# First part of a streaming encoder step: range checks placed by the scheduler, sample modulation and one weight's high halves on GpSimd

## The chip, the cores and the metric

The kernel runs on one core of one Trainium2 chip. The metric is the device time of one execution in microseconds. The core has five engines that run side by side, each through its own list of instructions in order: TensorE (PE in the profile), VectorE (DVE), ScalarE (ACT), GpSimd (POOL) and SyncE (SP, which only issues DMAs here). They wait for each other through semaphores.

## The reference

One layer of a hybrid encoder, for 1024 tokens of a prompt and 8 groups of 16 sample tokens (1152 tokens in all, model width 1024):

```python
mod = jax.nn.silu(c) @ w_ada + b_ada
shift, scale, gate = jnp.split(mod[:, None, :], 3, axis=-1)
h = rms_norm(x, norm_g) * (1 + scale) + shift
proj = h @ w_in
q, k, v, z_att, z_ssd, xbc, dt_raw, gates = jnp.split(proj, IN_SPLITS, axis=-1)
```

Attention over chunks with bands, a state-space scan and merge gates follow, and at the end an output projection and a residual add. The change lies in the part that makes `h` and the first pieces of `proj`.

## The kernel before

Matrix products run in half precision with both operands split in a high half (the value rounded to f16) and a low half (what the rounding left), so each product is three matmuls. Range checks go with that: `level` (L689) squares a tile on ScalarE and keeps a sum per row, and the sums are looked at only at the very end of the kernel. Nothing else waits for a `level`, except the reuse of the buffer that it reads.

The first part works through the model width in eighths, k = 0 to 7, in transposed form (width on the partitions, 1152 tokens along the row). Its steps for one k are:

- TensorE multiplies the conditioning by a slice of `w_ada` (`mod_a`, L1102), ScalarE copies the result out of PSUM (`mod_copy`, L1127), TensorE brings it into columns (`mod_b`, L1108), and ScalarE adds biases (`mod_c`, L1138 and L1139). Now shift and scale of this eighth are there, one column for the prompt and eight for the samples.
- VectorE normalises the tokens (`norm_x`, L1147). ScalarE applies scale and shift to the 1024 prompt tokens twice: as high half in f16 (`h_hi`, L1160) and in f32 (`h_rest`, L1165).
- For the 128 sample tokens the scale differs by group, so two tensor-tensor operations with broadcast columns do it (`h_samples`, L1156 and L1157). ScalarE rounds them to the high half (`h_smp`, L1169).
- VectorE takes the low half of all tokens (`h_low`, L1172: f32 minus high half).
- TensorE multiplies (`z_mm`, L1179, nine matmuls for each k) for the first projection, whose weight halves come from L1185 (ScalarE) and L1188 (VectorE).

Rounds k = 3, 4, 5 also split the three parts of the second weight: high halves by `w_high` (L1226, ScalarE), low halves by `w_low2` (L1232, VectorE), followed by a `level` of the raw part.

The second weight feeds `dense_tok` (L1023 to L1025): for each block of 128 tokens, eight triples of matmuls, one for each k. A triple needs the high and low halves of `h` for its k and the weight part that holds its columns. Blocks end in L1464 to L1470 (copies out of PSUM, squares, sums for the norms of q and k). GpSimd works out those norms (L1497, L654 to L659) and scales q and k (L1501), and TensorE transposes them (L1521). Splits of later weights are L697 (ScalarE) and L698 (VectorE); L679 and L1269 are loads of raw weights by SP.

The order on each engine is not the order of the code. A class `Order` goes through all instructions with a table of costs and gives out, for each engine, a fixed order. Instructions whose names are in `pinned` keep the written order on their engine; `late` puts them there, and the whole first part is written with `late`. Names in `fill` are put behind others:

```python
u["at"] = u["i"] + self.FILL * (u["ins"][0].name in self.fill) - self.FAST * u["fast"]
```

with FILL = 600 places of the written order; among the instructions that could go, the one with the smallest `at` is taken. The costs know nothing of one engine slowing another.

Of the kernel before, what the change touches and what calls it, by code (L numbers as in the profile page):

```python
# [13 lines left out]
AF = mybir.ActivationFunctionType  # L14
ALU = mybir.AluOpType

P = 128
# [3 lines left out]
NB = 8  # L21
NS = 16
# [37 lines left out]
SW = 2.0 ** 8  # L60
# [365 lines left out]
def trunk_kernel(ctx: ExitStack, tc: tile.TileContext, h, again):  # L426
    nc = tc.nc
# [101 lines left out]
    def alloc(lay, tag, cols):  # L529
        if lay is L_H or lay is L_W or lay is L_W3 or lay is L_Q or lay is L_V or lay is L_WQ or lay is L_WD:  # L530
            return Buf(arena, arena.alloc(lay, tag, cols // 2), cols, True)
        if lay is L_ST:
            return Buf(rarena, rarena.alloc(lay, tag, cols), cols)
        if (lay is L_SSD or lay is L_HEAD or lay is L_TAIL) and tag == "T" or lay is L_HEAD and tag == "Y":
            try:
                return Buf(arena, arena.alloc(L_MORE, "T", cols), cols)
            except NoSlot:
                pass
        return Buf(arena, arena.alloc(lay, tag, cols), cols)
# [90 lines left out]
    pinned, cuts, slow, fill, fast = set(), set(), set(), set(), set()  # L630
    pinning = [True]

    def late(x):
        if pinning[0]:
            pinned.add(x.ins.name)
        return x
# [26 lines left out]
    wraw, wsplit = {}, {}  # L663
# [21 lines left out]
    def level(x, scale, keep=lambda x: x, kind="w"):  # L685

        c, n = meant[kind], x.shape[-1]
        meant[kind] += 1
        keep(nc.scalar.activation(junk[:, :n], x, AF.Square, scale=scale * n ** -0.5, accum_out=sums[:, c:c + 1]))  # L689
# [346 lines left out]
    for k in range(KT):  # L1036
        b = alloc(L_START, "T", NT)
# [6 lines left out]
    def ada_load(k):  # L1044

        ws = [alloc(L_START, "ada", 1024) for i in range(2)]
        for i, w in enumerate(ws):
            dma(w.ap, h["wada1"][k][:, i * 1024:(i + 1) * 1024])
        wada.append(ws)
# [18 lines left out]
    hhi = [alloc(L_H, "h", NT) for _ in range(KT)]  # L1068
    hlo = [alloc(L_H, "h", NT) for _ in range(KT)]
    hops = list(zip(hhi, hlo))  # L1070
    m3 = modt.rearrange("p (j b) -> p j b", b=9)
    a3 = amod.rearrange("p (j b) -> p j b", b=9)
# [10 lines left out]
    for k in range(1, KT):  # L1083
# [5 lines left out]
        x = xs_in[k].ap  # L1089
# [26 lines left out]
    def mod_a(k, copy=True):  # L1116
        w = wada[k]
        ps = mp[k] = pg(256)
        ms[k] = alloc(L_START, "e", 256)
        mod_cols(ps, w, 256)  # L1120
        for x in w:
            x.free()
        if copy:
            mod_copy(k)

    def mod_copy(k):
        late(nc.scalar.activation(ms[k].ap, mp.pop(k), AF.Copy))  # L1127

    def mod_b(k):
        p2 = p2s[k] = pg(18)  # L1130
        me = ms.pop(k)
        mod_sum(p2, me.ap, (k, 8 + k))
        me.free()

    def mod_c(k):

        p2 = p2s.pop(k)
        late(nc.scalar.activation(m3[:, k, :], p2[:, :9], AF.Identity, bias=par["b_ada"][:, k:k + 1]))  # L1138
        late(nc.scalar.activation(a3[:, k, :], p2[:, 9:18], AF.Identity, scale=par["norm_g"][:, k:k + 1],  # L1139
                                  bias=par["b_ada"][:, 8 + k:9 + k]))  # L1140

    def samples(x):
        return x.ap[:, NP:].rearrange("p (b q) -> p b q", q=NS)

    def norm_x(k):
        x = xs_in[k]
        late(nc.vector.tensor_tensor(x.ap, x.ap, rbc.ap, ALU.mult))  # L1147
# [3 lines left out]
    def h_samples(k):  # L1151

        x, t = xs_in[k], alloc(L_START, "T", NT)
        ht[k] = t
        ts_ = samples(t)
        late(nc.vector.tensor_tensor(ts_, samples(x), a3[:, k, 1:].unsqueeze(2).to_broadcast([P, NB, NS]), ALU.mult))  # L1156
        late(nc.vector.tensor_tensor(ts_, ts_, m3[:, k, 1:].unsqueeze(2).to_broadcast([P, NB, NS]), ALU.add))  # L1157

    def h_hi(k, c):
        late(nc.scalar.activation(hhi[k].r[:, c], xs_in[k].ap[:, c], AF.Identity, scale=a3[:, k, 0:1], bias=m3[:, k, 0:1]))  # L1160

    def h_rest(k):

        x, t = xs_in[k], ht[k]
        late(nc.scalar.activation(t.ap[:, :NP], x.ap[:, :NP], AF.Identity, scale=a3[:, k, 0:1], bias=m3[:, k, 0:1]))  # L1165
        x.free()

    def h_smp(k):
        late(nc.scalar.activation(hhi[k].r[:, NP:], ht[k].ap[:, NP:], AF.Copy))  # L1169

    def h_low(k):
        late(nc.vector.tensor_tensor(hlo[k].r, ht[k].ap, hhi[k].ap, ALU.subtract))  # L1172
# [3 lines left out]
    def z_mm(k, wpart, hop, gs=(0, 1, 2)):  # L1176

        for g in gs:
            late(nc.tensor.matmul(first[g], w01[wpart].r[:, k * P:(k + 1) * P], hop[k].r[:, groups[g]],  # L1179
                                  start=k == 0 and wpart == 0 and hop is hhi, stop=k == KT - 1 and hop is hlo))  # L1180
# [6 lines left out]
    def w01_low(c):  # L1187
        late(nc.vector.scalar_tensor_tensor(w01[1].r[:, c], wraw[0].ap[:, c], SW, w01[0].ap[:, c], ALU.mult, ALU.subtract))  # L1188
# [13 lines left out]
    x = xs_in[0]  # L1202
# [13 lines left out]
    acc.free()  # L1216
    sq[1].free()
    h_samples(0)
    norm_x(1)
    h_smp(0)  # L1220
# [2 lines left out]


    def w_high(j):
        late(nc.scalar.activation(wsplit[1][0].r[:, j * 1024:(j + 1) * 1024], wraw[1 + j].ap, AF.Copy, scale=SW))  # L1226

    def w_low2(j):
        hi, lo, _ = wsplit[1]
        b = wraw.pop(1 + j)  # L1230
        c = slice(j * 1024, (j + 1) * 1024)
        late(nc.vector.scalar_tensor_tensor(lo.r[:, c], b.ap, SW, hi.ap[:, c], ALU.mult, ALU.subtract))  # L1232
        level(b.ap, SW, late)
        b.free()


    for k in range(KT):
        if k == 0:
            z_mm(0, 0, hhi, (0,))
            mod_a(1)  # L1240
            z_mm(0, 0, hhi, (1,))
            z_mm(0, 1, hhi, (0, 1))
            z_mm(0, 0, hhi, (2,))
            z_mm(0, 1, hhi, (2,))
            mod_b(1)
            h_rest(0)
            mod_c(1)
            mod_a(2, False)
            mod_a(3, False)
            h_low(0)  # L1250
            h_samples(1)
            h_hi(1, slice(0, NP))
            h_smp(1)
            mod_copy(2)
            h_rest(1)
            w01_low(slice(256, 1024))
            level(wraw[0].ap, SW, late)
            wraw.pop(0).free()
            z_mm(0, 0, hlo)
            mod_b(2)  # L1260
            mod_c(2)
            norm_x(2)

            for i in range(3):
                if i == 1:
                    ada_load(6)
                    ada_load(7)
                b = wraw[1 + i] = alloc(L_RAW, "raw", 1024)
                dma(b.ap, parts[1 + i])  # L1269
            loaded[0] = 4  # L1270
            hold[0] = False
        else:
            if k + 1 < KT:
                h_samples(k + 1)
                h_hi(k + 1, slice(0, NP))
            if k + 2 < KT:
                mod_copy(k + 2)
            if 2 < k < 6:
                w_high(k - 3)
            if k + 1 < KT:  # L1280
                h_smp(k + 1)
                h_rest(k + 1)
            h_low(k)
            z_mm(k, 0, hhi)
            z_mm(k, 1, hhi)
            if k + 3 < KT:
                mod_a(k + 3, False)
            if k + 2 < KT:
                mod_b(k + 2)
                mod_c(k + 2)  # L1290
                norm_x(k + 2)
            if 2 < k < 6:
                w_low2(k - 3)
            z_mm(k, 0, hlo)
        ht.pop(k).free()
        if k == 2:
            wsplit[1] = [alloc(L_W3, "w", 3 * 1024) for _ in range(2)] + [3]
# [33 lines left out]
    def pause(t):  # L1331
        yield from until(clock[0] + t)
# [101 lines left out]
    def h_level():  # L1434
        for k in range(KT):
            yield from pause(6000)
            level(hhi[k].r, 1.0, kind="x")

    urgent.append(ev_first())
    urgent.append(h_level())  # L1440
    zs = {0: z_first}

# [2736 lines left out]
def trunk(tc, h):  # L4179

    nc = tc.nc
    with tc.tile_pool(name="again", bufs=1) as pool:
        again = pool.tile([1, 1], I32, name="again")
        trunk_kernel(tc, h, again)
        redo = nc.values_load(again, min_val=0, max_val=1)
        with tc.If(redo > 0):
            general_kernel(tc, h)
# [151 lines left out]
```

## Time and profile before

| what | us |
|---|---|
| median of three timed runs | 1725.98 |
| lowest and highest of them | 1722.39 and 1729.38 |
| profiled execution, its own time | 1723.17 |
| its span | 1721.4 |
| TensorE busy | 1678.6 |
| VectorE busy | 1376.6 |
| ScalarE busy | 1058.1 |
| GpSimd busy | 369.1 |

The profile is of one execution. Its span runs from the first to the last instruction; 1.8 us lie around it. A row of a timeline has the start, the duration, the engine, the line and the operation, output and input with shapes, and in brackets the idle time of that engine just before, with what ended it. Rows of waits have the total, how often and the longest. Matmul durations overlap, so the time that one takes is read from the distance between starts.

### The profile page before, as it was taken

The page shows a single profiled execution, that of the slowest core. Times are in us where ns is not written, and L with a number is a line of the kernel's source. Part 1 is how long each engine was busy: PE and PEld are TensorE (multiplying, and loading weights), DVE is VectorE, ACT ScalarE, POOL GpSimd, SP SyncE. Part 2 cuts the span into 40 slices and gives each one's busy share as a digit, 9 for nine tenths or more (in the row PEclk, how much of TensorE's full clock was granted, in tenths as well). Part 3 has the DMA queues.
Part 4 walks back from the last instruction along what each step waited for, and adds up shares of the span by engine and source line. Part 5 has one row for each costly group of instructions (what it writes and reads, how often), then busy time and mean ns, then how long its engine had stood idle before and what let it go on. Part 6 is the DMA issues. An engine that isn't in the chain of part 4 may idle for free. (4 is left out here: it accounts for less than half of the span.)

```text
span 1721.4 us, 36659 instructions
## 1 busy us (share of the span) xinstructions
PE 1678.6 (98%) x14265; PEld 1120.4 (65%) x14265; DVE 1376.6 (80%) x2539; ACT 1058.1 (61%) x2123; POOL 369.1 (21%) x640
## 2 busy tenths in 40 slices
PE   7999999999999999999999999999999999999998
PEld 3556565556565556666666666666657777777776
DVE  6458767878877888889988998997798677888973
ACT  8766556566565668457655765665379665774550
POOL 0133233135133111322321232232212101010000
PEclk9999999999999999999999999999999999999999
DMA  9248789797978687676858867788756866687661
GB/s 383 82 122 210 170 228 225 168 232 187 219 219 192 165 199 221 181 221 199 194 172 263 241 194 238 235 216 268 284 198 221 274 240 234 232 287 264 224 212 65
DMA packets 299249, 369.16 MB, mean 214 GB/s; under 512 B 211692, under 2 KB 213368, under 8 KB 299064
## 3 DMA queue, kind: packets, MB, share of 16 engines
q1 hardware_dynamic: 282040, 307.65, 64.0%
q0 software_dynamic: 17024, 59.06, 9.3%
q8 instruction: 114, 1.87, 0.5%
q14 instruction: 71, 0.58, 0.1%
HBM read 244.08 MB, written 74.06 MB: 185 GB/s over the span
## 5 line engine op out<-in xcount | busy, mean ns | idle before, releaser
L970 PE MATMUL d<-arena 128*128 128x384 f16 x1320 | 432.0, 327 | 4.4 <-DVE arena L1986 2.0
L973 PE MATMUL d<-arena 128*128 128x384 f16 x1320 | 431.5, 327 | 1.2 <-DVE arena L698 1.2
L971 PE MATMUL d<-arena 128*128 128x384 f16 x1320 | 431.3, 327 | 0.0
L689 ACT ACTIVATE arena<-arena 128x1024 bf16<-128x1024 f32 (+4 forms) x217 | 199.2, 918 | 130.1 <-DMA arena<-in_wall_dram 88.2
L698 DVE SCALAR_TENSOR_TENSOR arena<-arena 128x1024 f16<-128x1024 f32 (+2 forms) x157 | 181.8, 1166 | 61.0 <-ACT arena L697 60.5
L697 ACT ACTIVATE arena<-arena 128x1024 f16<-128x1024 f32 (+2 forms) x157 | 155.4, 994 | 83.2 <-DMA arena<-sum_d 40.5
L970 PEld LDWEIGHTS <-arena 128*128 128x128 f16 x1320 | 129.2, 98 | 90.9 <-issue 12.1
L1023 PE MATMUL d<-arena 128*128 128x384 f16 (+1 forms) x568 | 187.0, 329 | 0.0
L1024 PE MATMUL d<-arena 128*128 128x384 f16 (+1 forms) x568 | 186.3, 328 | 0.0
L1025 PE MATMUL d<-arena 128*128 128x384 f16 (+1 forms) x568 | 186.2, 328 | 0.0
L973 PEld LDWEIGHTS <-arena 128*128 128x128 f16 x1320 | 129.0, 98 | 87.8 <-DVE arena L698 1.9
L971 PEld LDWEIGHTS <-arena 128*128 128x128 f16 x1320 | 129.1, 98 | 82.5 <-issue 5.8
L1569 ACT ACTIVATE arena<-arena 128x640 f32<-128x640 f32 (+4 forms) x144 | 100.8, 701 | 63.4 <-DVE arena L1572 63.0
L877 PEld LDWEIGHTS <-arena 128*128 128x128 f16 x1120 | 109.3, 98 | 39.7 <-issue 12.2
L878 PEld LDWEIGHTS <-arena 128*128 128x128 f16 x1120 | 109.3, 98 | 32.4 <-issue 4.3
L876 PEld LDWEIGHTS <-arena 128*128 128x128 f16 x1120 | 109.4, 98 | 29.3 <-issue 1.5
L876 PE MATMUL d<-arena 128*128 128x288 f16 x400 | 114.5, 286 | 5.9 <-DVE arena L901 3.9
L876 PE MATMUL g<-arena 128*128 128x288 f16 x400 | 114.5, 286 | 1.2 <-DVE arena L901 1.2
L877 PE MATMUL g<-arena 128*128 128x288 f16 x400 | 114.5, 286 | 1.2 <-DVE arena L2200 1.2
L877 PE MATMUL d<-arena 128*128 128x288 f16 x400 | 114.5, 286 | 0.2 <-DVE arena L2200 0.2
L878 PE MATMUL g<-arena 128*128 128x288 f16 x400 | 114.5, 286 | 0.0
L878 PE MATMUL d<-arena 128*128 128x288 f16 x400 | 114.5, 286 | 0.0
(277 smaller groups left out, 3521.8 us busy)
## 6 DMA issues: line engine op xcount, KB each, us to landing
arena<-in_quad_dram SPq DMA_DIRECT2D x80, 512.0 KB, 7.0
arena<-in_wall_dram SPq DMA_DIRECT2D x77, 512.0 KB, 5.2
sum_d<-arena POOLq DMA_DIRECT2D x40, 512.0 KB, 4.9
arena<-sum_d SPq DMA_DIRECT2D x40, 512.0 KB, 4.9
arena<-acs_d SPq DMA_DIRECT2D x32, 576.0 KB, 6.2
arena<-in_kc_dram SPq DMA_DIRECT2D x64, 256.0 KB, 4.4
arena<-in_vc_dram SPq DMA_DIRECT2D x64, 256.0 KB, 3.6
arena<-in_wada_dram SPq DMA_DIRECT2D x24, 512.0 KB, 3.7
```

Source lines behind the costliest of these rows:

```text
L689: keep(nc.scalar.activation(junk[:, :n], x, AF.Square, scale=scale * n ** -0.5, accum_out=sums[:, c:c + 1]))
L697: keep(nc.scalar.activation(hi, x, AF.Copy, scale=scale))
L698: keep(nc.vector.scalar_tensor_tensor(lo, x, scale, hi, ALU.mult, ALU.subtract))
L876: nc.tensor.matmul(ps, wh, xh[:, c], start=first and k == 0, stop=False, skip_group_check=not first)
L877: nc.tensor.matmul(ps, wh, xl[:, c], start=False, stop=False, skip_group_check=not first)
L878: nc.tensor.matmul(ps, wl, xh[:, c], start=False, stop=k == 3, skip_group_check=not first)
L970: nc.tensor.matmul(ps, hi.r[:, wc], kh.r[:, tok], start=k == 0, stop=False)
L971: nc.tensor.matmul(ps, hi.r[:, wc], kl.r[:, tok], start=False, stop=False)
L973: nc.tensor.matmul(ps, lo.r[:, wc], kh.r[:, tok], start=False, stop=k == nk - 1)
L1023: nc.tensor.matmul(ps, kh.r[:, tok], wh, start=k == 0, stop=False)
L1024: nc.tensor.matmul(ps, kh.r[:, tok], wl, start=False, stop=False)
L1025: nc.tensor.matmul(ps, kl.r[:, tok], wh, start=False, stop=k == KT - 1)
```

## The change

The sample tokens' scale and shift (`h_samples`) are done by GpSimd and not by VectorE. The high halves of the second weight (`w_high`) are done by GpSimd, as a multiplication, and not by ScalarE. Three groups of range checks are no longer pinned but given to the scheduler as `fill`: that of the first weight, those of the three parts of the second weight, and those of the eight high halves of `h` (which were not pinned before, but not in `fill` either).

```diff
@@ -1153,8 +1153,8 @@
         x, t = xs_in[k], alloc(L_START, "T", NT)
         ht[k] = t
         ts_ = samples(t)
-        late(nc.vector.tensor_tensor(ts_, samples(x), a3[:, k, 1:].unsqueeze(2).to_broadcast([P, NB, NS]), ALU.mult))
-        late(nc.vector.tensor_tensor(ts_, ts_, m3[:, k, 1:].unsqueeze(2).to_broadcast([P, NB, NS]), ALU.add))
+        late(nc.gpsimd.tensor_tensor(ts_, samples(x), a3[:, k, 1:].unsqueeze(2).to_broadcast([P, NB, NS]), ALU.mult))
+        late(nc.gpsimd.tensor_tensor(ts_, ts_, m3[:, k, 1:].unsqueeze(2).to_broadcast([P, NB, NS]), ALU.add))
@@ -1223,14 +1223,14 @@
     def w_high(j):
-        late(nc.scalar.activation(wsplit[1][0].r[:, j * 1024:(j + 1) * 1024], wraw[1 + j].ap, AF.Copy, scale=SW))
+        late(nc.gpsimd.tensor_scalar(wsplit[1][0].r[:, j * 1024:(j + 1) * 1024], wraw[1 + j].ap, SW, None, ALU.mult))
 
     def w_low2(j):
         hi, lo, _ = wsplit[1]
         b = wraw.pop(1 + j)
         c = slice(j * 1024, (j + 1) * 1024)
         late(nc.vector.scalar_tensor_tensor(lo.r[:, c], b.ap, SW, hi.ap[:, c], ALU.mult, ALU.subtract))
-        level(b.ap, SW, late)
+        level(b.ap, SW, lambda x: fill.add(x.ins.name))
         b.free()
@@ -1254,7 +1254,7 @@
             w01_low(slice(256, 1024))
-            level(wraw[0].ap, SW, late)
+            level(wraw[0].ap, SW, lambda x: fill.add(x.ins.name))
             wraw.pop(0).free()
@@ -1434,7 +1434,7 @@
     def h_level():
         for k in range(KT):
             yield from pause(6000)
-            level(hhi[k].r, 1.0, kind="x")
+            level(hhi[k].r, 1.0, lambda x: fill.add(x.ins.name), kind="x")
```

The rounds of the loop in which these stand:

```python
            if 2 < k < 6:
                w_high(k - 3)
            if k + 1 < KT:
                h_smp(k + 1)
                h_rest(k + 1)
            h_low(k)
```

## The prediction

> **What bounds the kernel now.** I read the page first, then TensorE's waits, then the first 70 us engine by engine as timelines. The page says that TensorE is busy nearly all the time:
>
> ```profile
> span 1721.4 us, 36659 instructions
> PE 1678.6 (98%) x14265; PEld 1120.4 (65%) x14265; DVE 1376.6 (80%) x2539; ACT 1058.1 (61%) x2123; POOL 369.1 (21%) x640
> ```
>
> So an edit off TensorE pays only by what it takes from or adds to TensorE's idle time. Between 14 and 100 us the waits of TensorE that this change can reach are two:
>
> ```profile
> PE g L1108 <- ACT arena L1127: 2.0, 4, 1.3
> PE g L1521 <- POOL arena L1501: 1.0, 1, 1.0
> ```
>
> Three microseconds are all that a quicker first part could win. The timeline of ScalarE shows who paces that part. Its rounds, one for each eighth of the model width, begin with L1138 (start, duration, engine, line; in brackets idle time before it):
>
> ```profile
> 21.98 0.27 ACT L1138 ACTIVATE arena<-g,arena 128x9 f32<-128x9 f32 x1 [0.28 <-PE g L1108]
> ...
> 30.62 1.04 ACT L689 ACTIVATE arena<-arena 128x1024 bf16<-128x1024 f32 x1
> ...
> 31.66 0.25 ACT L1138 ACTIVATE arena<-g,arena 128x9 f32<-128x9 f32 x1
> ...
> 34.93 0.25 ACT L1138 ACTIVATE arena<-g,arena 128x9 f32<-128x9 f32 x1
> 35.08 0.35 ACT L1139 ACTIVATE arena<-g,arena 128x9 f32<-128x9 f32 x1
> 35.46 1.24 ACT L1160 ACTIVATE arena<-arena 128x1024 f16<-128x1024 f32 x1
> 36.61 0.36 ACT L1127 ACTIVATE arena<-g 128x256 f32<-128x256 f32 x1
> 36.87 0.30 ACT L1169 ACTIVATE arena<-arena 128x128 f16<-128x128 f32 x1
> 37.07 1.23 ACT L1165 ACTIVATE arena<-arena 128x1024 f32<-128x1024 f32 x1
> 38.21 0.25 ACT L1138 ACTIVATE arena<-g,arena 128x9 f32<-128x9 f32 x1
> ...
> 40.16 1.04 ACT L1226 ACTIVATE arena<-arena 128x1024 f16<-128x1024 f32 x1
> ...
> 42.43 0.25 ACT L1138 ACTIVATE arena<-g,arena 128x9 f32<-128x9 f32 x1
> ...
> 47.54 0.26 ACT L1138 ACTIVATE arena<-g,arena 128x9 f32<-128x9 f32 x1
> ...
> 52.64 0.27 ACT L1138 ACTIVATE arena<-g,arena 128x9 f32<-128x9 f32 x1
> ```
>
> The rounds take 3.27, 3.28, 4.22, 5.11 and 5.10 us with no gap: ScalarE bounds them, and L1226 (1.04) and L689 (1.04) make the last three long. VectorE in the same stretch:
>
> ```profile
> 33.99 1.35 DVE L1147 TENSOR_TENSOR arena<-arena 128x1152 f32<-128x1152 f32 x1
> 35.46 0.29 DVE L1156 TENSOR_TENSOR arena<-arena 128x128 f32<-128x128 f32 x1
> ...
> 36.00 1.35 DVE L1172 TENSOR_TENSOR arena<-arena 128x1152 f16<-128x1152 f32 x1
> 37.27 1.35 DVE L1147 TENSOR_TENSOR arena<-arena 128x1152 f32<-128x1152 f32 x1
> ```
>
> L1172 to L1147 is 1.27 us from start to start. TensorE idles little in such a round, 0.18 us before L1108, so it has 3.1 us of work for 3.28; the later rows give the spacing of matmuls, 0.163 us, and the end of a tile:
>
> ```profile
> 37.03 0.61 PE L1108 MATMUL g<-arena 128*128 128x9 f32 x4 [0.18 <-ACT arena L1127]
> ...
> 61.19 0.33 PE L1024 MATMUL g<-arena 128*128 128x384 f16 x1
> 61.35 0.33 PE L1025 MATMUL g<-arena 128*128 128x384 f16 x1
> ...
> 65.30 0.33 PE L1025 MATMUL d<-arena 128*128 128x384 f16 x1
> ```
>
> **What the change moves.** On ScalarE, at the head of the loop, the first weight's range check (L689) now stands before the first L1138:
>
> ```order
>  L1127 ACTIVATE arena<-g_175 128x256
>  L1185 ACTIVATE arena<-arena 128x1024
> +L689 ACTIVATE arena<-arena 128x1024
>  L1138 ACTIVATE arena<-g_193,arena 128x9
>  L1139 ACTIVATE arena<-g_193,arena 128x9
> ```
>
> It leaves the place at 30.62 us. Its 1.04 us has 0.28 us of idle time to hide in, so the first L1138 comes 0.76 us later, and the third is relieved of 1.04.
>
> On VectorE, in the rounds of the weight's low halves (L1232), the sample steps L1156 and L1157 go:
>
> ```order
>  L1232 SCALAR_TENSOR_TENSOR arena<-arena 128x1024
> -L1156 TENSOR_TENSOR arena<-arena 128x128
> -L1157 TENSOR_TENSOR arena<-arena 128x128
>  L1172 TENSOR_TENSOR arena<-arena 128x1152
>  L1147 TENSOR_TENSOR arena<-arena 128x1152
>  L1232 SCALAR_TENSOR_TENSOR arena<-arena 128x1024
> -L1156 TENSOR_TENSOR arena<-arena 128x128
> -L1157 TENSOR_TENSOR arena<-arena 128x128
>  L1172 TENSOR_TENSOR arena<-arena 128x1152
> ```
>
> On GpSimd they appear, with the high halves L1226 between them:
>
> ```order
> +L1226 TENSOR_SCALAR arena<-arena 128x1024
> +L1156 TENSOR_TENSOR arena<-arena 128x128
> +L1157 TENSOR_TENSOR arena<-arena 128x128
> +L1226 TENSOR_SCALAR arena<-arena 128x1024
> +L1156 TENSOR_TENSOR arena<-arena 128x128
> +L1157 TENSOR_TENSOR arena<-arena 128x128
> +L1226 TENSOR_SCALAR arena<-arena 128x1024
> +L1156 TENSOR_TENSOR arena<-arena 128x128
> +L1157 TENSOR_TENSOR arena<-arena 128x128
> ```
>
> Before, GpSimd stood idle there:
>
> ```profile
> 70.73 0.20 POOL L1497 TENSOR_SCALAR arena<-arena 128x16 f32<-128x16 f32 x1 [69.36 <-DVE arena L1470]
> ...
> 76.88 1.90 POOL L1501 TENSOR_TENSOR arena<-arena 128x1024 f32<-128x1024 f32 x1
> ```
>
> So ScalarE's L1169 and all behind it now wait for GpSimd's L1157, and VectorE's L1232 for GpSimd's L1226. The question is what GpSimd takes beside a busy VectorE. The trace of before answers it from later attention work (GpSimd's rows, then VectorE's):
>
> ```profile
> 144.10 1.52 POOL L656 TENSOR_TENSOR arena<-arena 128x16 f32<-128x16 f32 x1
> 145.70 0.22 POOL L657 TENSOR_TENSOR arena<-arena 128x16 f32<-128x16 f32 x1
> ...
> 146.88 1.18 POOL L657 TENSOR_TENSOR arena<-arena 128x16 f32<-128x16 f32 x1
> 148.16 1.05 POOL L658 TENSOR_SCALAR arena<-arena 128x16 f32<-128x16 f32 x1
> 149.29 1.07 POOL L659 TENSOR_TENSOR arena<-arena 128x16 f32<-128x16 f32 x1
> ```
>
> ```profile
> 146.77 3.51 DVE L698 SCALAR_TENSOR_TENSOR arena<-arena 128x1024 f16<-128x1024 f32 x3
> ```
>
> While VectorE runs three operations that read two SBUF tiles back to back, three GpSimd operations that take 0.22 us elsewhere take 1.1 us each: each ends only when the VectorE operation beside it ends. The other direction:
>
> ```profile
> 491.57 1.03 DVE L698 SCALAR_TENSOR_TENSOR arena<-arena 128x832 f16<-128x832 f32 x1 [0.23 <-ACT arena L697]
> 493.23 2.35 DVE L698 SCALAR_TENSOR_TENSOR arena<-arena 128x832 f16<-128x832 f32 x1 [0.64 <-ACT arena L697]
> ```
>
> ```profile
> 492.80 1.90 POOL L1501 TENSOR_TENSOR arena<-arena 128x1024 f32<-128x1024 f32 x1
> ```
>
> A VectorE operation of 1.03 us that starts 0.43 us into a GpSimd operation of 1.90 takes 2.35: it lost 1.32 of the 1.47 us that GpSimd had left. The Trainium skill, "SBUF — State Buffer", section "Who interferes with whom", states the rule that speaks against this change: a VectorE instruction with two SBUF inputs and a GpSimd instruction that reads SBUF exclude each other for the whole instruction. By it the loss would be all 1.47, by the row a tenth less; I go by the row.
>
> L1147, L1172, L1188 and L1232 all read two SBUF tiles, so the two engines take turns in every round.
>
> Prices of the new GpSimd operations. The form row gives a second size of L1501:
>
> ```profile
> L1501 POOL TENSOR_TENSOR arena<-arena 128x256 f32<-128x256 f32 x8 | 5.0, 628 | 0.2
> ```
>
> From 0.63 us at 256 columns and 1.90 at 1024 follow 1.65 ns a column and 0.2 us fixed: 0.41 us at 128 columns, of which 0.1 can pass before the turn comes. I take 0.35, bounds 0.30 and 0.41. No row shows L1226 on GpSimd: 1.90 (L1501, the same engine and columns, two operands) bounds it above and 1.04 (ScalarE's L1226) below; I take 1.5, the middle, since it reads one operand and nothing shows what the second costs. The Trainium skill, "GPSIMD Reference", section "Engine selection", calls one-input work roughly line rate; with the clock and lanes of its section "Specifications" my estimate is 0.85 us and the 0.2 fixed, 1.05 in all, and the sum would be 1.35 us smaller. No run here shows it yet.
>
> *Round by round.* The new ring: L1165 ends, L1172 1.27, GpSimd 0.35, L1147 1.27 (it waited for its turn), GpSimd 0.35, ScalarE's L1169 0.20 and L1165 1.24, three or four hand-overs of 0.03: 4.8 us, where ScalarE alone took 3.28. ScalarE's other items (L1160, L1127, a remaining L689) fit in its new idle time, so moving the checks and L1226 off it is worth nothing here. In the first such turn L1157 comes behind L1172 and L1188: L1169 is about 0.9 us later on top of the 0.76. By the third L1138: 0.76 + 0.9 - 1.04 = +0.6. Two rounds of 4.8 against 3.27 and 3.28: +3.0. One against 4.22: +0.6. Then two with weights, where nothing of VectorE and GpSimd overlaps: 1.27 + 1.27 + 1.14 + 1.5 + 0.7 = 5.9 against 5.11 and 5.10, +1.6. The L1138 of 52.64 us comes at about 58.4.
>
> *On TensorE.* The plan fills the rounds with triples of L1023 to L1025, but these need the weight's parts (L1232) and stand in a fixed order; a wait for one holds all behind it. The third L1232 starts with that L1138 and takes 1.2 us, so the triple that needs it starts at about 59.8. Up to the last row that closes the common part (before, the triple at 61.35) TensorE has 17 triples of three times 0.163 us, 8.3, and 0.4 for the last L1172: 68.5 instead of 61.7, **+6.8 us**.
>
> *Given back at L1521.* Before, the tile that TensorE ended at 65.30 was taken out of PSUM only at
>
> ```profile
> 69.35 0.36 ACT L1464 ACTIVATE arena<-d 128x256 f32<-128x256 f32 x1
> ```
>
> behind checks on ScalarE, and GpSimd's norm chain, from the 70.73 row to the end of the 76.88 row, was what L1521 waited 1.0 us for. Now L1521 stands six matmuls earlier on TensorE (d_671 and d_717 are PSUM tiles of the same projection):
>
> ```order
> -L1023 LDWEIGHTS arena
> -L1023 MATMUL d_717<-arena 128x384
> -L1024 LDWEIGHTS arena
> -L1024 MATMUL d_717<-arena 128x384
> -L1025 LDWEIGHTS arena
> -L1025 MATMUL d_717<-arena 128x384
>  L1521 MATMUL g_690<-arena 128x128 x4
>  L1521 MATMUL g_703<-arena 128x128 x4
> +L1023 LDWEIGHTS arena
> +L1023 MATMUL d_671<-arena 128x384
> +L1024 LDWEIGHTS arena
> +L1024 MATMUL d_671<-arena 128x384
> ```
>
> That takes 1 us of cover away; but ScalarE, which has done more checks by then, follows that tile within about 1.5 us instead of 4. The wait goes: **-1.0**. If not, it is 0.
>
> *At nothing:* the 16 sample steps taken off VectorE (its end is set by turns), the third weight load on SP that passes one bias and one cache load (0.33 us each to issue, used after 100 us), GpSimd's set-up row that now precedes L1156 (GpSimd is idle until then). Behind row 130 or so of each engine the order is unchanged, and TensorE has no cover, so the delay stays to the end.
>
> *Sum:* +6.8 - 1.0 = +5.8 on the profiled execution's own 1723.17 us, 1729.0. The three timed runs have the median 1725.98, 2.8 above it; on that scale **1731.8 us**. Bounds: 0.30 and 1.04 for the two prices take off 0.6 and 1.4, 0.41 and 1.90 add 0.4 and 1.2: +3.8 to +7.4, and +8.4 if L1521 still waits.
>
> **Rivals.**
> - *No turns to speak of*: GpSimd gets both sample steps in while VectorE waits for ScalarE anyway. Then ScalarE's rounds shrink by L1226 and L689, TensorE is rid of at most the 2.0 + 1.0 us above, of which I take 1.8 (the rounds before 31 us keep their waits): 1724.2. Against it stand the rows at 146.88 to 149.29. For it: a GpSimd row sometimes comes free of VectorE (145.70). Decides: whether L1156 and L1157 stay under 0.5 us.
> - *Worse turns*: the row at 144.10 lasted 1.52 us, past one VectorE boundary into the next. If L1226 loses two turns in each of its three rounds, 1.27 more each, 3.8 in all, less 0.6 where VectorE would idle: +9, 1735. Decides: L1226 above 2.5 us.
> - *Given back later*: TensorE's few later waits absorb part of the delay: +2, 1728.
>
> **Chances.** Forecast 0.62, no turns 0.14, worse turns 0.16, given back 0.08. Over 0.5% is over 8.6 us, about what a measurement can tell from no change; the timed runs alone spread by 7. Slower: 0.14 of the worse turns and 0.08 of the forecast's upper end, 0.22. Faster: 0.02 from no turns. Within: 0.76. The range leaves out half of the no-turns case and a little above the worse turns: 1724 to 1737.5.
>
> **What would show it.** L1156, L1157 on GpSimd at 0.4 us alone and 1.2 to 1.6 beside L1147 or L1172; L1147 stretched where L1226 runs; gaps in ScalarE's rounds before L1169, released by GpSimd; rounds of about 4.8 and 5.9 us; the triple of 61.35 at about 68; no wait at L1521. It is wrong if rounds stay at 3.3 us, if L1226 takes under 1 us, or if the delay at 100 us is not there at the end.

## The result, and the profile after

The changed kernel takes 1732.09 us (median of 13 runs, 1724.58 to 1738.23) against 1726.3 us before (13 runs, 1722.23 to 1731.5). The ratio is 1.0035, 95% interval 1.0019 to 1.005: about 6 us slower, inside the 0.5% that was called no change, and 0.3 us from the forecast of 1731.8. The total is right. What follows asks whether its terms were, and three of them were not.

The page of the changed kernel, its first line and the row of engines:

```profile
span 1731.8 us, 36667 instructions
PE 1686.0 (97%) x14265; PEld 1125.8 (65%) x14265; DVE 1374.5 (79%) x2523; ACT 1058.0 (61%) x2120; POOL 405.7 (23%) x659
```

The share of TensorE falls by one point, while GpSimd gains 37 us of busy time. GpSimd's timeline after (start, duration, engine, line, operation; in brackets idle time before it and what ended it) shows where these are:

```profile
24.49 0.40 POOL L1156 TENSOR_TENSOR arena<-arena 128x128 f32<-128x128 f32 x1 [23.12 <-DVE arena L1209]
24.97 0.40 POOL L1157 TENSOR_TENSOR arena<-arena 128x128 f32<-128x128 f32 x1
...
33.11 1.22 POOL L1156 TENSOR_TENSOR arena<-arena 128x128 f32<-128x128 f32 x1 [2.23 <-ACT arena L1139]
34.41 1.40 POOL L1157 TENSOR_TENSOR arena<-arena 128x128 f32<-128x128 f32 x1
...
45.10 2.78 POOL L1226 TENSOR_SCALAR arena<-arena 128x1024 f16<-128x1024 f32 x1
47.86 0.39 POOL L1156 TENSOR_TENSOR arena<-arena 128x128 f32<-128x128 f32 x1
48.34 1.27 POOL L1157 TENSOR_TENSOR arena<-arena 128x128 f32<-128x128 f32 x1
49.58 3.87 POOL L1226 TENSOR_SCALAR arena<-arena 128x1024 f16<-128x1024 f32 x1
```

A sample step takes 0.40 us when VectorE is idle, as at 24.49, and 1.0 to 1.4 us when it has to wait for one of VectorE's operations. L1226 takes 2.78 us even alone (at 45.10; VectorE stands idle until 47.92). VectorE's timeline after, for two of the same rounds and the third L1232:

```profile
32.71 1.36 DVE L1172 TENSOR_TENSOR arena<-arena 128x1152 f16<-128x1152 f32 x1 [0.61 <-issue]
33.99 1.56 DVE L1147 TENSOR_TENSOR arena<-arena 128x1152 f32<-128x1152 f32 x1
...
47.92 1.43 DVE L1232 SCALAR_TENSOR_TENSOR arena<-arena 128x1024 f16<-128x1024 f32 x1 [3.06 <-POOL arena L1226]
49.27 1.55 DVE L1172 TENSOR_TENSOR arena<-arena 128x1152 f16<-128x1152 f32 x1
50.74 2.19 DVE L1147 TENSOR_TENSOR arena<-arena 128x1152 f32<-128x1152 f32 x1
53.48 1.42 DVE L1232 SCALAR_TENSOR_TENSOR arena<-arena 128x1024 f16<-128x1024 f32 x1 [0.55 <-POOL arena L1226]
...
59.04 1.42 DVE L1232 SCALAR_TENSOR_TENSOR arena<-arena 128x1024 f16<-128x1024 f32 x1 [0.55 <-POOL arena L1226]
```

Read the two fences against each other by ends. L1156 ends at 34.33, 0.26 us after L1172 (34.07). L1147 was issued at 33.99, takes 0.21 us longer than the 1.35 of before and ends at 35.55. L1157, issued at 34.41, ends at 35.81, again 0.26 later. That is the turn-taking. ScalarE waits for the end of it (its timeline after):

```profile
32.53 0.26 ACT L1138 ACTIVATE arena<-g,arena 128x9 f32<-128x9 f32 x1
...
35.84 0.31 ACT L1169 ACTIVATE arena<-arena 128x128 f16<-128x128 f32 x1 [1.27 <-POOL arena L1157]
...
52.03 0.25 ACT L1138 ACTIVATE arena<-g,arena 128x9 f32<-128x9 f32 x1
...
57.77 0.27 ACT L1138 ACTIVATE arena<-g,arena 128x9 f32<-128x9 f32 x1
```

In all, L1138 starts at 27.97, 32.53, 37.19, 41.84, 46.50, 52.03 and 57.77: rounds of 4.56, 4.66, 4.65, 4.66, 5.53 and 5.74 us. TensorE's waits after, between 14 and 100 us:

```profile
PE g L1108 <- ACT arena L1127: 4.0, 3, 2.2
PE d L1024 <- DVE arena L1232: 1.3, 2, 1.1
```

and the triple that needs the third L1232 (60.51), the one that closes the common part (68.64), and L1521, the first L1537 and the first L1389 behind them (timeline of TensorE after; the first L1102 row is where this part begins on TensorE, 0.38 us later than before):

```profile
19.61 1.07 PE L1102 MATMUL g<-arena 128*32 128x256 f32 x16
...
60.51 0.32 PE L1024 MATMUL d<-arena 128*128 128x384 f16 x1 [0.16 <-DVE arena L1232]
...
68.64 0.33 PE L1025 MATMUL g<-arena 128*128 128x384 f16 x1
...
101.11 1.09 PE L1521 MATMUL g<-arena 128*128 128x128 f32 x8 [0.55 <-POOL arena L1501]
...
109.84 0.38 PE L1537 MATMUL g<-arena 128*128 128x128 f32 x2
...
831.38 0.85 PE L1389 MATMUL g<-arena 128*32 128x384 f32 x6
```

The same three end rows of before:

```profile
19.23 1.07 PE L1102 MATMUL g<-arena 128*32 128x256 f32 x16
...
103.06 0.38 PE L1537 MATMUL g<-arena 128*128 128x128 f32 x2
...
824.63 0.85 PE L1389 MATMUL g<-arena 128*32 128x384 f32 x6
```

I use the distance from the first L1102 to the first L1537 on TensorE as the **marker** of what the first part costs: 103.06 - 19.23 = 83.83 us before, 109.84 - 19.61 = 90.23 after, +6.40. The delay stays: the first L1389, a good 700 us later, is 6.75 us behind that of before, or 6.37 without the later start.

The two profiled spans differ by 10.4, and to read that as the cost of the change would be wrong. The rest comes after the L1389, where in two stretches the granted clock (PEclk, the column before the two of the DMAs) was lower in the execution of after. The windows of after and, second, of before:

```profile
850.00:920.00 70.00, 66.89 (x467) 41.76 (x465) 56.95 (x79) 35.10 (x61) 19.57 (x30) 0.98 0.58 189
...
1500.00:1700.00 200.00, 194.20 (x1559) 153.50 (x1557) 162.30 (x243) 112.18 (x193) 7.00 (x13) 0.98 0.68 234
```

```profile
850.00:920.00 70.00, 67.36 (x533) 44.88 (x531) 58.79 (x92) 36.44 (x65) 15.75 (x29) 1.00 0.62 197
...
1500.00:1700.00 200.00, 193.23 (x1573) 153.29 (x1571) 158.04 (x240) 105.94 (x185) 5.40 (x10) 1.00 0.66 225
```

A kernel with a marker of only +0.48 (checks and weight, below) had the clock 0.98 and 0.97 in the same two stretches and a span of 1732.4. So a single span says little here; the marker and the timed medians agree with each other (+6.4 and +5.8).

### The profile page after: what moved, and what is told of

The parts are those of the page before. It is cut to its first block, busy times and chain, and to the rows that moved or that the text cites. A ratio compares the mean times of both kernels' runs of the same rounds, so it can differ in the third digit from the quotient of the medians.

```text
span 1731.8 us, 36667 instructions
## 1 busy us (share of the span) xinstructions
PE 1686.0 (97%) x14265; PEld 1125.8 (65%) x14265; DVE 1374.5 (79%) x2523; ACT 1058.0 (61%) x2120; POOL 405.7 (23%) x659
## 4 chain that ended last, share of the span: by engine, by line
PE 57%; DVE 13%; DMA 10%; issue 9%; ACT 7%; POOL 3%; SPq 0%; POOLq 0%; ACTq 0%; DVEq 0%
PE d L970 6%; PE d L973 6%; PE d L971 6%; PE d L1023 5%; PE d L1024 5%; PE d L1025 5%; PE g L1629 2%; DMA arena<-acs_d 2%; ACT arena L689 2%; DVE arena L1827 2%; DMA arena<-in_quad_dram 1%; DMA arena<-in_wall_dram 1%; DMA arena<-arena 1%; PE d L876 1%; PE g L878 1%
## 5 line engine op out<-in xcount | busy, mean ns | idle before, releaser
L689 ACT ACTIVATE arena<-arena 128x1024 bf16<-128x1024 f32 (+4 forms) x217 | 199.1, 917 | 118.9 <-DMA arena<-in_wall_dram 74.9
```

## The experiments

Theory, as in the prediction: GpSimd's operations that read SBUF and VectorE's operations with two SBUF inputs take turns, the sample steps sit in ScalarE's ring, and this is the loss. Rivals: the moved checks (level ahead of the first L1138, other places later) cost the time, or the price of L1226 on GpSimd does. All edits below are against the kernel before, unless they say otherwise. The marker is read from each run's own TensorE rows. Each is from one execution, and how far it scatters from one to the next was not measured, so a few tenths are not read as an effect.

| run | checks | samples | weight | marker | against before | timed ratio, 95% interval |
|---|---|---|---|---|---|---|
| after | moved | GpSimd | GpSimd | 90.23 | +6.40 | 1.0035, 1.0019 to 1.005 |
| e1 | moved | - | - | 87.52 | +3.69 | 1.0018, 0.9998 to 1.0037 |
| e2 | - | GpSimd | - | 86.35 | +2.52 | 1.0014, 0.9994 to 1.0035 |
| e3 | - | - | GpSimd | 84.32 | +0.49 | 0.9991, 0.9969 to 1.0012 |
| e4 | moved | memsets | GpSimd | 82.69 | -1.14 | only its start is read |
| e5 | moved | - | GpSimd | 84.31 | +0.48 | 0.9995, 0.9972 to 1.0018 |
| e6 | - | GpSimd | GpSimd | 89.62 | +5.79 | profile only |
| e7 | moved | GpSimd | - | 88.16 | +4.33 | profile only |
| e8 | - | L1157 alone | - | 84.86 | +1.03 | profile only |
| e9 | high halves of h | - | - | 84.48 | +0.65 | 1.0003, 0.9976 to 1.003 |
| e10 | weight blocks | - | - | 87.05 | +3.22 | 1.0, 0.9973 to 1.0027 |

**The parts alone: e1, e2, e3.** The checks:

```diff
-        level(b.ap, SW, late)
+        level(b.ap, SW, lambda x: fill.add(x.ins.name))
-            level(wraw[0].ap, SW, late)
+            level(wraw[0].ap, SW, lambda x: fill.add(x.ins.name))
-            level(hhi[k].r, 1.0, kind="x")
+            level(hhi[k].r, 1.0, lambda x: fill.add(x.ins.name), kind="x")
```

> The range checks alone: all three groups go to the scheduler, GpSimd does nothing of the first part. Marker: the time on TensorE from the first L1102 to the first L1537 row; before 83.83 us, the changed kernel 90.23 (+6.40). Theory of turns (VectorE and GpSimd exclude each other, and that is the whole loss): nothing is lost here, rounds of ScalarE stay at 3.3 us and the weight rounds fall from 5.1 to about 4.2, marker 82.8 to 83.8. Rival, the checks' new places cost (the first stands ahead of the first L1138, +0.66 us, others ahead of PSUM copies): marker 84.3 to 85.5.

The samples:

```diff
-        late(nc.vector.tensor_tensor(ts_, samples(x), ..., ALU.mult))
-        late(nc.vector.tensor_tensor(ts_, ts_, ..., ALU.add))
+        late(nc.gpsimd.tensor_tensor(ts_, samples(x), ..., ALU.mult))
+        late(nc.gpsimd.tensor_tensor(ts_, ts_, ..., ALU.add))
```

> The sample steps alone on GpSimd; high halves and checks as before. Theory of turns: rounds without weights take 4.66 us as in the changed kernel, L1226 and L689 on ScalarE hide in its waits for GpSimd, weight rounds 4.7 to 5.2; marker 87.3 to 88.5 (+3.5 to +4.7). Rival, the slow L1226 on GpSimd (2.8 us and more) is most of the loss: marker 84 to 85.5.

The weight's high halves:

```diff
-        late(nc.scalar.activation(wsplit[1][0].r[...], wraw[1 + j].ap, AF.Copy, scale=SW))
+        late(nc.gpsimd.tensor_scalar(wsplit[1][0].r[...], wraw[1 + j].ap, SW, None, ALU.mult))
```

> The high halves alone on GpSimd; sample steps and checks as before. Theory of turns: L1226 takes 2.8 us on GpSimd but is early, since nothing else is queued there, and holds VectorE only while it reads; ScalarE's weight rounds fall from 5.1 to about 4.2; marker 83.0 to 84.2. Rival, the slow L1226 is the loss: VectorE's L1232 waits for it in each of three rounds, marker 85.5 to 88.

e3 (84.32) lies 0.1 above the range of the theory and far from the rival: L1226 alone on GpSimd costs some 0.5 us in this execution, and not all of that need be its own. In e3 the granted clock between 35 and 40 us was 0.69, and ScalarE's L1138 at 39.22 waited 0.74 us for TensorE's L1108. e2 (86.35) lies between the two, 1 us under the theory. In it the rounds are 3.90, 4.65, 4.67, 5.10 and 5.11 us: the last two are as before, because there ScalarE still has L1226 and L689 to do while GpSimd takes its turns. One of the sample steps also came free:

```profile
33.41 1.46 POOL L1156 TENSOR_TENSOR arena<-arena 128x128 f32<-128x128 f32 x1 [3.26 <-DVE arena L1172]
34.94 0.40 POOL L1157 TENSOR_TENSOR arena<-arena 128x128 f32<-128x128 f32 x1
```

e1 (87.52) was expected by neither: the marker grew by 3.69 with GpSimd untouched. Its rounds on ScalarE without weights are 3.3 us, as the theory had it (L1138 at 31.30, 34.63 and 37.91). The row that closes the common part comes at 61.24, against 61.35 before, so up to there nothing is lost. The loss is in one place behind it, at 64 us (TensorE's timeline, then ScalarE's, of e1):

```profile
64.38 0.32 PE L1023 MATMUL d<-arena 128*128 128x384 f16 x1 [2.82 <-ACT arena L1465]
...
65.08 0.52 PE L1023 MATMUL d<-arena 128*128 128x384 f16 x1
65.40 0.52 PE L1024 MATMUL d<-arena 128*128 128x384 f16 x1
```

```profile
59.54 1.16 ACT L689 ACTIVATE arena<-arena 128x1152 bf16<-128x1152 f16 x1
...
60.83 1.17 ACT L689 ACTIVATE arena<-arena 128x1152 bf16<-128x1152 f16 x1
...
62.10 1.28 ACT L1311 ACT_TABLE_LOAD   x1
63.40 0.49 ACT L1311 ACTIVATE arena<-d 128x384 f32<-128x384 f32 x1
63.78 0.38 ACT L1464 ACTIVATE arena<-d 128x256 f32<-128x256 f32 x1
```

TensorE waits for a PSUM tile that L1464 and L1465 empty. Before, the last item ahead of the first L1464 (60.99) is the check at 59.83, which corresponds to the one at 59.54 here. In e1 ScalarE's plan has put one check more, a table load and L1311 in between. Behind that wait ten matmuls come 0.32 us apart instead of 0.16, which adds about 1.6 us to the 2.8; some of it comes back later. The changed kernel and those with two of its parts (e5, e6, e7) have the table load behind the first two L1464, as before:

```profile
67.00 0.37 ACT L1464 ACTIVATE arena<-d 128x256 f32<-128x256 f32 x1
...
67.72 0.38 ACT L1464 ACTIVATE arena<-d 128x256 f32<-128x256 f32 x1
...
68.60 1.28 ACT L1311 ACT_TABLE_LOAD   x1
```

(ScalarE's timeline after). So e1's loss is not a part of the 6.4, and the parts can't be read off kernels that hold one of them alone.

**The pairs: e5, e6, e7.** Each is the changed kernel with one part put back: e5 has the samples on VectorE again, e6 the checks in written order, e7 L1226 on ScalarE.

> The changed kernel with the sample steps back on VectorE: range checks to the scheduler and the high halves on GpSimd. Theory of turns: without sample steps on GpSimd there is one operation in each weight round that takes turns, and only while it reads, so rounds without weights take 3.3 us and the marker (TensorE, first L1102 to first L1537) is 82.7 to 84.3, against 83.83 before and 90.23 in the changed kernel. Rival, the checks' places or the slow L1226 carry a part of their own: marker above 86. On ScalarE the table load of L1311 stands behind the first two copies out of PSUM (L1464) here, so the wait that the checks alone showed should not come.

> Sample steps and high halves on GpSimd, all checks where they were. Theory of turns: as the changed kernel, first L1138 0.66 us earlier but one check of 1.04 back in the third round; rounds 4.7, 4.7, 4.7, then 5.5 to 5.8; marker 89 to 90.8. Rival, the checks in the scheduler's hands carry the loss: marker below 87.

> Checks to the scheduler and sample steps on GpSimd, high halves on ScalarE. Theory of turns: rounds of 4.7 without weights, 4.8 to 5.1 with; marker 86 to 87.5, some 3 us less than the changed kernel since L1226 on GpSimd stands ahead of sample steps there. Rival, only the reads of the sample steps matter and L1226 is free: marker 89.5 or more, as the changed kernel.

e6 (89.62) is in its range. e5 (84.31) and e7 (88.16) agree with the theory in direction, e5 at the edge of its range and e7 0.7 above it (there the first L1521 waits 1.0 us for GpSimd, as before). Read from the changed kernel: the samples cost 90.23 - 84.31 = 5.9 us, the weight 90.23 - 88.16 = 2.1, the checks 0.6. They add up to more than 6.4, since they share a cost: without the checks, the samples alone cost 2.52 and the weight alone 0.49, but both 5.79. Both engines' rows above say why. With the two together, GpSimd's in-order list is sample steps, L1226, sample steps. L1226 starts only when L1157 has had its turn, L1232 waits for it (3.06 us idle at 47.92), and TensorE's triples wait for L1232. e6 shows besides that a lower granted clock is not the loss: it was 1.00 in all the windows from 15 to 110 us, while the changed kernel had 0.73 and 0.66 in two of them.

**The turns themselves: e4 and e8.** e4 is the changed kernel with the two sample steps as GpSimd operations that only write:

```diff
-        late(nc.gpsimd.tensor_tensor(ts_, samples(x), ..., ALU.mult))
-        late(nc.gpsimd.tensor_tensor(ts_, ts_, ..., ALU.add))
+        late(nc.gpsimd.memset(ts_, 0.5))
+        late(nc.gpsimd.memset(ts_, 0.25))
```

> The changed kernel with each of the two sample steps replaced by a GpSimd memset of the same 128 columns, which reads nothing; the sample tokens' scale and shift are left out (their values are a constant). The memsets do not wait for L1139. Theory of turns: L1169 no longer waits for GpSimd, rounds without weights 3.3 us, marker 83 to 85. Rival, a hop over a third engine and L1226 are the loss, not SBUF reads: marker above 87.

Its constant values send the kernel down a longer path of its own later on, so only the first 110 us are read. GpSimd's list and VectorE's timeline in e4:

```profile
46.37 3.52 POOL L1226 TENSOR_SCALAR arena<-arena 128x1024 f16<-128x1024 f32 x1
49.84 0.20 POOL L1156 MEMSET arena<- 128x128 f32 x1
50.10 0.21 POOL L1157 MEMSET arena<- 128x128 f32 x1
```

```profile
49.29 1.34 DVE L1147 TENSOR_TENSOR arena<-arena 128x1152 f32<-128x1152 f32 x1
```

L1138 is back at 3.28 us a round (27.86, 31.15, 34.43, 37.71), and the marker is 7.5 us less than the changed kernel's, a little below the expected 83. The queue and the engine of the steps are the same, but two things are gone: the reads of SBUF, and the waits, since a memset needs neither L1139 nor L1147 and in these rounds no L1169 waits for GpSimd. So e4 shows that the whole loss of the rounds hangs on ScalarE's wait for GpSimd; it does not tell the turn from the way over a third engine.

The rows of the changed kernel tell the two apart. Its L1156 starts at 33.11. At the 0.40 us of the rows at 24.49 and 24.97, both steps would have ended at about 34.0. ScalarE was ready for L1169 at 34.57 (35.84 less the 1.27 of idle time). By this estimate the way over GpSimd would have cost nothing there. The steps took 1.22 and 1.40 us instead, each ending 0.26 us behind an operation of VectorE, and the wait of 1.27 is most of the 1.38 that a round lost. So it is the waiting for a turn, not the work, that cost the time.

The Trainium skill, "SBUF — State Buffer", section "Who interferes with whom", says that a VectorE instruction with two SBUF inputs contends with GpSimd's reads and not with an operation that only writes; e4's rows agree (0.20 and 0.21 us beside VectorE's L1147, which takes 1.34, and 1.35 elsewhere).

e8 is the kernel before with half the dose, L1157 alone on GpSimd:

```diff
-        late(nc.vector.tensor_tensor(ts_, ts_, ..., ALU.add))
+        late(nc.gpsimd.tensor_tensor(ts_, ts_, ..., ALU.add))
```

> Only the second sample step (L1157, the add) on GpSimd, the first stays on VectorE, all else as before. Theory of turns: one turn in each round in place of two: the round is low half 1.27, first step 0.33, one turn behind L1147 1.27, 0.35, 0.20, 1.24, about 4.7 if the GpSimd step misses the gap before L1147, and 3.4 to 3.6 if it gets it; marker 84 to 86.4. Rival, the hop to GpSimd itself (two semaphores and its fixed 0.2 us) is the cost: marker 83.9 to 84.3, rounds 3.3.

```profile
37.36 1.45 POOL L1157 TENSOR_TENSOR arena<-arena 128x128 f32<-128x128 f32 x1 [2.28 <-DVE arena L1156]
41.09 1.45 POOL L1157 TENSOR_TENSOR arena<-arena 128x128 f32<-128x128 f32 x1 [2.28 <-DVE arena L1156]
```

One turn each round, 1.45 us long; the rounds between 32.72 and 40.19 take 3.74 and 3.73 us, where two turns make 4.66 and none 3.28. That lies between the two values expected: the step got the gap before L1147, but it ends late enough that L1169 still waits 0.34 us for it. The marker, 84.86, is in the range of the turns alone (+1.03).

**What moved checks cost: e9, e10.** e9 moves only the last of the three kinds of check of e1's diff (high halves of h), e10 only the first two (weight blocks).

> Only the checks of the modulated tiles' high halves go to the scheduler; the checks of the weight blocks stay in written order, GpSimd as before. In ScalarE's order the first two L1464 then stand ahead of L1311's table load, as before. Theory (what the run with all checks moved lost at 64 us is the place of the table load ahead of the first copies out of PSUM, not the move of the checks): no wait of TensorE for L1465 over 1 us there, and the marker, TensorE's time from the first L1102 to the first L1537, is 82.8 to 84.6. Rival (moving checks costs wherever it is done, since they come back later in front of other work): marker above 86, as with all checks moved (87.5).

> Only the checks of the weight blocks go to the scheduler, the checks of the high halves stay in written order, GpSimd as before. In ScalarE's order the table load of L1311 now stands ahead of the first L1464. Theory (the place of the table load costs): TensorE waits 2 to 3.5 us for L1465 near 64 us, marker 86.5 to 88.5. Rival (it is the checks themselves that stand ahead of the copies; here fewer are moved): the wait is under 1.5 us, marker below 85.5.

Both came as the theory had them, 84.48 and 87.05. TensorE's wait in e10:

```profile
64.70 0.44 PE L1023 MATMUL d<-arena 128*128 128x384 f16 x1 [2.81 <-ACT arena L1465]
```

In e9 no such wait exists and the table load (62.91) follows the two L1464 (61.31, 62.04). So what costs is what stands ahead of the first copies out of PSUM, and which checks are free decides where the plan puts it. It is not the table load alone: from the check at 61.15 to L1464 at 64.10 e10's rows have 2.95 us, 1.3 for that check and 1.7 for the table load and L1311, and no run parts these two. Nor does the place cost in every plan: e4 has the table load ahead of the first L1464 too (59.21 and 60.89), but ScalarE is there some 3 us earlier than in e1 and e10, and TensorE waits 0.29 us. The timings of e1 and e10 can't confirm their +3.7 and +3.2: both intervals hold these and no change as well.

No version is shown to beat the kernel before: e3 and e5, the best by time, have 1 inside their intervals.

## Why the prediction was right, point by point

**Turns in ScalarE's rounds: right, in mechanism and size.** 4.8 us a round forecast, 4.66 measured. L1165 to L1165 goes over L1172, GpSimd, L1147, GpSimd, L1169, each waiting for the one before. With half the dose (e8) the excess falls from 1.38 to 0.45, and where no L1169 waits for GpSimd (e4) the rounds return to 3.28.

**The first rounds: right.** The first L1138 comes at 23.02 instead of 21.98, of which 0.38 is the later start: +0.66 for the check ahead of it, 0.76 forecast. The third, 32.53 against 31.66, is +0.49 after the same correction, +0.6 forecast.

**The price of L1226: wrong, outside its bounds.** "I take 1.5", bounds 1.04 and 1.90, from a two-operand GpSimd operation of the same number of columns. It takes 2.78 alone and up to 3.9 beside VectorE. The argument that one operand cannot cost more than two was the fault: L1501 writes f32 and L1226 writes f16, and no row of GpSimd in the trace of before writes f16. Whether it is the output type or the operation was not tried. The Trainium skill's "roughly line rate" for one-input work ("GPSIMD Engine Reference", "Engine selection"), from which I had 1.05, is further off still.

**Two weight rounds of 5.9, "where nothing of VectorE and GpSimd overlaps": wrong, the other way.** L1226 from 49.58 to 53.45 runs beside L1147 (50.74 to 52.93), and L1147 takes 2.19 where 1.35 is its own time: it lost 0.84 us to an operation of 2.78. If both had excluded each other to the end, L1147 would have ended at about 54.8. So the rounds came to 5.5 and 5.7 instead of 5.9. The two errors cancelled: the operation is 1.3 us longer than I took, and the rounds are 0.2 to 0.4 shorter, so the overlap gave back 1.5 to 1.7. The rival "worse turns" set its point of decision at L1226 above 2.5 us; the point was passed, and the +9 did not come, for this reason.

**TensorE's closing triple: right in time, not in its path.** The last row of it is at 68.64 instead of 61.35, 7.3 later; 0.38 of it is the later start, so +6.9 against +6.8. But the two steps that lead there were off, in opposite directions. The L1138 of 52.64 came at 57.77 and not at 58.4, since the rounds were shorter. And the third L1232 did not start with it: the prediction left out that it waits for the third L1226. It started at 59.04, 1.27 us later, and took 1.42 us instead of 1.2, so the triple that needs it started at 60.51 against 59.8. That the sum of these is right is luck. TensorE's waits on the way there are 4.0 us at L1108, 2.0 before, and a new 1.3 for L1232.

**Given back at L1521: half.** -1.0 was forecast. The first L1521 indeed no longer waits, but a later one, which had no wait before, waits 0.55 us for the same GpSimd step (101.11). From the closing triple's +6.9 to the marker's +6.4 there are 0.5 us. The cover that I set at nothing for later tiles was not there for all of them.

**Moved checks "worth nothing here": right for the changed kernel,** where putting them back gains 0.6 us, but not as a rule: e1 and e10 lose over 3 us of the marker by the same edits with another plan around them. That the order behind the first part stays the same was read from the changed kernel's order, and holds for it.

**The sum:** +6.9 - 0.5 on TensorE, and the timed runs show +5.8. A forecast of +5.8 was on the mark since the errors, of up to 1.3 us, were of both signs: that it is within 0.3 us is luck, that turns on the sample steps cost several us is not. The bounds were loose in one place: the 1.4 and 1.2 for the price of L1226 count it three times, where the sum has it in two rounds.

## What to carry to other kernels

Before work moves from VectorE to an idle GpSimd, list what VectorE runs beside it: if those operations read two SBUF tiles, a 0.4-us step can last as long as a whole VectorE operation, and if the step is in the ring that paces a stage, it can cost that in every round. Price a moved operation by a row of the same operation and output type as well as the same size, and keep the bounds wide where there is none. When a scheduler places part of the work, a part tested alone gets another plan, so pairs (the whole with one part put back) say more than single parts, and a marker on the busiest engine shows several us where total times do not.

## What the runs showed of the hardware

- GpSimd's L1226 (128x1024, f32 to f16, one operand) takes 2.78 us alone, and an L1147 of VectorE beside it lost only 0.84: its hold on the other engine is shorter than its duration. The rows of e3 below point to a hold at its start. VectorE's L1157, which takes 0.29 us elsewhere in e3, starts 0.28 us into an L1226 and takes 1.01. Less its own 0.29, its end at 36.98 puts the release at about 36.7, an estimate of 1.0 us after the L1226 began.

```profile
35.69 2.88 POOL L1226 TENSOR_SCALAR arena<-arena 128x1024 f16<-128x1024 f32 x1 [34.31 <-DMA arena<-in_wall_dram]
```

```profile
35.97 1.01 DVE L1157 TENSOR_TENSOR arena<-arena 128x128 f32<-128x128 f32 x1
```

- An operation of GpSimd that only writes (memset 128x128, 0.20 us) did not stretch VectorE's two-input operations, nor they it.
- Behind a TensorE wait of 2.8 us the granted clock was lower for some microseconds: in e1 matmuls come 0.32 us apart instead of 0.16 from about 64.8 to 68.0 us. In the changed kernel the windows from 30 to 35 and from 45 to 50 us have 0.73 and 0.66, and L1102 takes 1.94 us (1.07 else). That is hidden there by waits that end later (L1232's, at 54.95 and 60.51). The Trainium skill, "TensorE: Matmul & The Clock Gate", section "Part 1: The HAM clock gate (the "warmup" mystery)", has TensorE fall to half its clock after an idle window of about 3.4 us; the half speed agrees, but the wait ahead of e1's dip was only 2.82. In e2 a wait of 2.07 us, at 30.39, had a clock of 1.00 behind it. Whether the idle time brings the dip was not tested.

```profile
33.83 1.94 PE L1102 MATMUL g<-arena 128*32 128x256 f32 x16
...
37.71 1.07 PE L1102 MATMUL g<-arena 128*32 128x256 f32 x16
```
